# Probabilities times values in two float32r passes instead of float32 halves

## The chip, the cores and the metric

The kernel runs on one core of one Trainium2 chip. The metric is the device time of one execution in microseconds (us): lower is better. A run is repeated, and the median counts.

## The reference, cut to what matters

Two layers of a decoder trunk over 512 tokens of width 1024. In each layer four branches (a gated convolution, a sparse attention, a gated recurrence called HGRN2, and an attention to 256 memory tokens) start from one projection of the normalised input, are lifted to the full width, gated, summed and projected out; a feed-forward part follows. The change lies in the sparse attention. Each of its 8 heads has 64 dimensions, and all heads share one key and one value head:

```python
def one_block(args):                                # 128 queries
    qb, iqb, iwb, qpos = args
    ...
    _, sel = lax.top_k(score, topk)                 # 128 keys for each query
    ...
    logits = jnp.where(valid[:, :, None, :], logits, -jnp.inf)
    p = jax.nn.softmax(logits, axis=-1).astype(v.dtype)
    return jnp.einsum('bthk,btkd->bthd', p, v_sel)  # probabilities times values
```

Everything is float32, and the result has to be close to a float32 computation.

## The kernel before, in words

**Numbers in two parts.** Most matrix products take both operands apart into a high part, rounded to float32r, and a low part, what the rounding left. `mm3` (lines 267 to 272) adds three float32r products in PSUM: high by high, high by low, low by high. These are the lines L270 to L272 that fill the profile. Weights come in chunks of 1024 KB or 512 KB; for each half of a chunk ScalarE rounds the high part (`w_hi`) and VectorE subtracts (`w_lo`, line 225), at a high priority (`AHEAD`). All ScalarE activations go through the helper `A`, so they carry line 97 and are told apart by their tiles.

**The sparse attention.** `attend` (lines 688 to 721) makes eight steps in each layer: four blocks of 128 queries (t = 0 to 3), and two groups q of four heads for each. A step works on t+1 blocks of 128 keys, b = 0 to t, since later keys are masked. For each of its four heads it multiplies queries and keys (L685, L686, into a PSUM tile "at"), adds the bias that masks the keys not selected and takes the row's extreme value on VectorE (L698), takes the exponential and the sum on ScalarE, the reciprocal on VectorE (L701), and scales on ScalarE. Then, for each block of keys, four transposes on TensorE (L709) put the four heads' probabilities side by side in a PSUM tile "tr" of 512 columns, and ScalarE copies it to the SBUF tile `pt`. Last, the values: for each block and each half e of the four heads one float32 matmul of 256 columns (L715) with the values `vt` (128 keys by 64 dimensions) as weights; e = 0 writes partitions 0 to 63 of `pv`, e = 1 partitions 64 to 127, so that two heads lie above two others. In the profile each of these 80 matmuls is two instructions. ScalarE rounds `pv` to `y_hi`, VectorE subtracts to `y_lo` (line 720); the lift of branch B reads them. `vt` is written by ScalarE in `c_kv` (line 787), once for each block of tokens.

**What sets the order.** The kernel is written in generators: `weave` (line 851) runs one step of the lift of branch A or of the recurrence's values, then R2 = 3 attend steps, and so on. A scheduler in the tile framework then orders the instructions of each engine by its own model of time, with the waits put in as semaphores; from there each engine works through its own queue in order. Every PSUM or SBUF tile is one of a few buffers under a name, and a new tile waits until the one before it in the same buffer has been read: three "mm" tiles in PSUM for projections (MM_BUFS), three "tr", two "at". SBUF is reused as well: the pool of the recurrence (`hgrn`, line 853) lies where the attention's pools lay. The recurrence begins with `logits` (lines 873 to 881): six chunks of projections whose products with `r_b` on VectorE (L880) read an "mm" tile and write `zf`, `zq` and `zg`; the first `zf` tiles of each layer lie over the attention's `pt` buffers, in the kernel before as in the changed one.

Of the kernel before, what the change touches and what calls it, by code (L numbers as in the profile page):

```python
# [12 lines left out]
F32 = mybir.dt.float32  # L13
F32R = mybir.dt.float32r
I32 = mybir.dt.int32
U8 = mybir.dt.uint8
AF = mybir.ActivationFunctionType
OP = mybir.AluOpType
# [3 lines left out]
P = 128  # L22
S = 512
NT = S // P
# [4 lines left out]
HD = 64  # L29
# [20 lines left out]
HG = ["zzzHHlHlHzzzHHHHll", "zzzHHHHllzzzHHHllH"]  # L50
WARM = 14
LOOK = ["0000", "0010"]
W_BUFS, RAW_BUFS, G_BUFS, PT_BUFS, PR_BUFS = 3, 2, 4, 2, 5
MV_BUFS, MP_BUFS = 1, 3
R1, R2 = 6, 3

# [13 lines left out]
def hybrid_trunk(ctx: ExitStack, tc: tile.TileContext, x, mem, positions, norm_mix, w_in, conv_w,  # L70
# [3 lines left out]
    act, dve, pe, pool = nc.scalar, nc.vector, nc.tensor, nc.gpsimd  # L74

    consts = ctx.enter_context(tc.tile_pool(name="consts", bufs=1))
    start = ctx.enter_context(ExitStack())
# [12 lines left out]
    def A(dst, src, func, **kw):  # L90
        name = tables.get(func)
        if name is not None and name != table["set"]:
            load = act.preload_act_table_set(name)
            for u in table["users"]:
                tc.add_manual_dep(load.ins, u.name, order, reason="table set")
            table.update(set=name, load=load.ins, users=[])
        i = act.activation(dst, src, func, **kw)  # L97
        if name is not None:
            tc.add_manual_dep(i.ins, table["load"].name, order, reason="table set")
            table["users"].append(i.ins)  # L100
        return i
# [4 lines left out]
    def at_ps():  # L106
        return pat.tile([P, 512], F32, name="at", bufs=AT_BUFS)

    def tr_ps():
        return pat.tile([P, 512], F32, name="tr", bufs=TR_BUFS)  # L110

    def f(ap):
        return ap.bitcast(F32)
# [28 lines left out]
    ps = tr_ps()  # L142
# [16 lines left out]
    ps = tr_ps()  # L159
# [20 lines left out]
    for l in range(DEPTH):  # L180
        a = sp.tile([P, HD], F32, name=f"gq_raw{l}")
# [5 lines left out]
        b = consts.tile([P, HD], F32, name=f"gk{l}")  # L187
# [14 lines left out]
    def small(n, name="small", bufs=12):  # L202
        return consts.tile([P, 8], F32, name=name, bufs=bufs)[:, :n]
# [297 lines left out]
    def mixer(l, h, norms, cm, cf):  # L501
        mix = cm.enter_context(tc.tile_pool(name="mix", bufs=1, side="right"))
        r_t, r_b = norms()
# [172 lines left out]
        with pool_("dsa") as dp:  # L676
            qS = dp.tile([P, 8, S], F32R, name="qS")
            kS = (dp.tile([P, S], F32R, name="k_hi"), dp.tile([P, S], F32R, name="k_lo"))
            pool.memset(f(kS[1][HD:P, :]), 0.0)
            vt = dp.tile([P, NT, HD], F32, name="vt")  # L680
            biases = [causal_bias] + [dp.tile([P, (t + 1) * P], F32, name=f"bias{t}") for t in range(1, NT)]

            def dots(ps, q, k, hh, t, n):
                s = slice(t * P, (t + 1) * P)
                pe.matmul(ps, q[:, hh, s], k[0][:, :n], start=True, stop=False)  # L685
                pe.matmul(ps, q[:, hh, s], k[1][:, :n], start=False, stop=True)  # L686

            def attend(t, dp2, y_b):
                n = (t + 1) * P
                s = slice(t * P, (t + 1) * P)  # L690
                for q in range(2):
                    probs = []
                    for i in range(4):
                        ps = at_ps()[:, :n]
                        dots(ps, qS, kS, 4 * q + i, t, n)
                        p = dp2.tile([P, S], F32, name="prob", bufs=PR_BUFS)[:, :n]
                        mx, sm = small(1), small(1)
                        dve.tensor_tensor_reduce(out=p, in0=ps, in1=biases[t], scale=-1.0, scalar=-OFF * 4,  # L698
                                                 op0=OP.add, op1=OP.min, accum_out=mx)
                        A(p, p, AF.Exp, bias=mx, scale=-1.0, accum_out=sm)  # L700
                        dve.reciprocal(sm, sm)  # L701
                        A(p, p, AF.Copy, scale=sm)
                        probs.append(p)
                    pt = dp2.tile([P, NT, S], F32, name="pt", bufs=PT_BUFS)
                    for b in range(t + 1):
                        pp = tr_ps()
                        for e in range(2):
                            for i in range(2):
                                pe.transpose(pp[:, (2 * e + i) * P:(2 * e + i + 1) * P],  # L709
                                             probs[2 * i + e][:, b * P:(b + 1) * P], ident)  # L710
                        A(pt[:, b, :], pp, AF.Copy)
                    pv = tr_ps()[:, :2 * P]
                    for b in range(t + 1):
                        for e in range(2):
                            pe.matmul(pv[e * HD:(e + 1) * HD, :], vt[:, b, :], pt[:, b, e * 2 * P:(e + 1) * 2 * P],  # L715
                                      start=b == 0, stop=b == t)
                    pv = pv.rearrange("p (a b) -> p a b", b=P)
                    hi, lo = (y_b[x][:, 2 * q:2 * q + 2, s] for x in range(2))
                    A(hi, pv, AF.Copy)
                    dve.tensor_sub(lo, pv, f(hi))  # L720
                    yield

            with pool_("idx") as ip:
# [44 lines left out]
                def twin(ps, t, c0, norm, dst):  # L768
                    u = ip.tile([P, 2, HD], F32, name="twin", bufs=2)
                    A(u[:, 0, :], ps[:, c0:c0 + HD], AF.Copy, scale=r_t[:, t:t + 1])  # L770
                    if norm:
                        headnorm(u[:, 0:1], 1, gk_b[l])
                    rope(u[:, 0:1], 1, t)
                    dve.tensor_copy(u[:, 1, :], u[:, 0, :])
                    ps = tr_ps()[:, :P]
                    pe.transpose(ps, u.rearrange("p a b -> p (a b)"), ident)
                    s = slice(t * P, (t + 1) * P)
                    A(dst[0][:, s], ps, AF.Copy)
                    dve.tensor_sub(dst[1][0:HD, s], ps[0:HD], f(dst[0][0:HD, s]))

                def iq_part(ps, t, c0, heads, h0):
                    u = unit(ps, t, c0, heads)
                    rope(u, heads, t)
                    heads_T(iqS, h0, u.rearrange("p a b -> p (a b)"), heads, t)

                def c_kv(ps, t):
                    A(vt[:, t, :], ps[:, 64:128], AF.Copy, scale=r_t[:, t:t + 1])
                    twin(ps, t, 0, True, kS)
                    iq_part(ps, t, 128, 2, 0)

# [39 lines left out]
                def projections():  # L830
                    for c0, n, handle in ((C_DK, 256, c_kv), (C_DK + 256, 256, c_iq), (C_DK + 512, 200, c_last),
                                          (C_DQ, 256, c_q(0)), (C_DQ + 256, 256, c_q(1))):
                        w = wchunk(w_in[l][:, c0:c0 + n], KD, n)
                        for t in range(NT):
                            ps = mm_ps()[:, :n]
                            tokens(w, h, t, ps)
                            handle(ps, t)
                        yield
# [11 lines left out]
            with pool_("att", "left") as dp2:  # L850
                weave(chain(lift(0, y_a, merged), values(hv)), chain(*(attend(t, dp2, y_b) for t in range(NT))), R2)
# [229 lines left out]
    for l in range(DEPTH):  # L1081
        with ExitStack() as ctx_ffn:
            with ExitStack() as ctx_mix:
                h, ssq, xT = mixer(l, h, (lambda: (norm_token(ssq), norm_feature(ssq))) if l else (lambda: norms),
                                   ctx_mix, ctx_ffn)
            h, ssq = ffn(l, h, ssq, xT)
# [29 lines left out]
```

## Time and profile before

| | us |
|---|---|
| Median of three runs (2047.63 to 2047.9) | 2047.9 |
| The profiled execution | 2047.48 |
| Its span, first to last instruction | 2045.4 |
| TensorE busy | 2034.5 |
| VectorE busy | 1269.3 |
| ScalarE busy | 1017.5 |
| Sparse attention with what is woven into it, layer 0 | about 340 to 470 |
| The same, layer 1 | about 1300 to 1440 |

How to read the views: a row of the timeline gives the start in us from the beginning of the span, the duration, the engine, the line and the operation, the tiles (out<-in), the shapes, how many instructions it merges, and in brackets how long the engine had been idle and who ended that. A row of the groups gives line, engine, operation, tiles and shapes with the count, then busy us and the mean in ns, then the idle time just before, with its releasers. A row of the windows gives a stretch, its length, the busy time of each engine with its count (PE, PEld, DVE, ACT, POOL), the granted TensorE clock, the share of the DMA engines and GB/s. PE is TensorE, PEld its weight loads, DVE VectorE, ACT ScalarE, POOL GpSimd. Matmuls are pipelined and their ends are modelled: the distance of two starts says more than the printed duration.

### The profile page before, as it was taken

The page shows a single profiled execution, that of the slowest core. Times are in us where ns is not written, and L with a number is a line of the kernel's source. Part 1 is how long each engine was busy: PE and PEld are TensorE (multiplying, and loading weights), DVE is VectorE, ACT ScalarE, POOL GpSimd, SP SyncE. Part 2 cuts the span into 40 slices and gives each one's busy share as a digit, 9 for nine tenths or more (in the row PEclk, how much of TensorE's full clock was granted, in tenths as well). Part 3 has the DMA queues.
Part 4 walks back from the last instruction along what each step waited for, and adds up shares of the span by engine and source line. Part 5 has one row for each costly group of instructions (what it writes and reads, how often), then busy time and mean ns, then how long its engine had stood idle before and what let it go on. Part 6 is the DMA issues. An engine that isn't in the chain of part 4 may idle for free.

```text
span 2045.4 us, 26581 instructions
## 1 busy us (share of the span) xinstructions
PE 2034.5 (99%) x10348; PEld 1715.8 (84%) x10348; DVE 1269.3 (62%) x2507; ACT 1017.5 (50%) x1834; POOL 9.8 (0%) x33
## 2 busy tenths in 40 slices
PE   8999999999999999999999999999999999999999
PEld 8998988888888888888889898888888888888887
DVE  6779998547676544334457889963777754533442
ACT  7653655766665423223355456576767633322331
POOL 0000000000000000000000000000000000000000
PEclk9999999999999999999999999999999999999999
DMA  7632232223233232233243213322223322323322
GB/s 253 220 89 94 68 93 93 64 71 93 78 118 113 83 103 93 93 105 102 87 155 94 88 58 107 97 76 63 83 83 101 126 90 96 103 75 111 97 79 93
DMA packets 187709, 203.79 MB, mean 100 GB/s; under 512 B 4270, under 2 KB 176384, under 8 KB 187456
## 3 DMA queue, kind: packets, MB, share of 16 engines
q1 hardware_dynamic: 183872, 193.56, 29.8%
q10 hardware_dynamic: 3552, 8.41, 1.1%
q8 instruction: 81, 1.33, 0.3%
q14 instruction: 44, 0.36, 0.1%
q0 software_dynamic: 160, 0.13, 0.0%
HBM read 191.60 MB, written 10.49 MB: 99 GB/s over the span
## 4 chain that ended last, share of the span: by engine, by line
PE 99%; DMA 1%; DVE 0%; ACT 0%; SPq 0%; issue 0%; DVEq 0%
PE mm L270 30%; PE mm L272 30%; PE mm L271 30%; PE tr L715 1%; PE tr L709 1%; PE at L686 1%; PE at L685 1%; PE at L272 1%; PE at L270 1%; PE at L271 1%; DMA w_raw<-in_mem_w_kv_dram 1%; PE at L963 0%; PE at L937 0%; PE tr L653 0%; PE tr L754 0%; PE tr L972 0%
## 5 line engine op out<-in xcount | busy, mean ns | idle before, releaser
L270 PE MATMUL mm<-h_hi,w_hi 128*128 128x512 f32 x1664 | 653.0, 393 | 0.0
L271 PE MATMUL mm<-h_lo,w_hi 128*128 128x512 f32 x1664 | 652.1, 392 | 0.0
L272 PE MATMUL mm<-h_hi,w_lo 128*128 128x512 f32 x1664 | 650.1, 392 | 0.0
L225 DVE TENSOR_TENSOR w_lo<-w_raw,w_hi 128x1024 fp32r<-128x1024 f32 (+1 forms) x346 | 419.5, 1213 | 364.5 <-ACT w_hi L97 361.3
L97 ACT ACTIVATE w_hi<-w_raw 128x1024 fp32r<-128x1024 f32 (+1 forms) x346 | 363.4, 1051 | 460.8 <-PE mm L271 414.5
L272 PEld LDWEIGHTS mm<-h_hi,w_lo 128*128 128x128 f32 x1664 | 312.8, 188 | 64.8 <-issue 1.2
L270 PEld LDWEIGHTS mm<-h_hi,w_hi 128*128 128x128 f32 x1664 | 312.8, 188 | 64.5 <-issue 2.2
L271 PEld LDWEIGHTS mm<-h_lo,w_hi 128*128 128x128 f32 x1664 | 312.9, 188 | 63.8 <-issue 2.0
L272 PE MATMUL mm<-w_hi,h_lo 128*128 128x256 f32 (+1 forms) x448 | 128.2, 286 | 0.0
L271 PE MATMUL mm<-w_lo,h_hi 128*128 128x256 f32 (+1 forms) x448 | 127.0, 285 | 0.0
L270 PE MATMUL mm<-w_hi,h_hi 128*128 128x256 f32 (+1 forms) x448 | 127.0, 285 | 0.0
L271 PE MATMUL mm<-a_lo,w_hi 128*128 128x512 f32 x272 | 106.3, 391 | 0.0
L270 PE MATMUL mm<-a_hi,w_hi 128*128 128x512 f32 x272 | 106.0, 390 | 0.0
L272 PE MATMUL mm<-a_hi,w_lo 128*128 128x512 f32 x272 | 105.8, 391 | 0.0
L270 PE MATMUL mm<-y_hi,w_hi 128*128 128x512 f32 x256 | 101.4, 397 | 0.0
L272 PE MATMUL mm<-y_hi,w_lo 128*128 128x512 f32 x256 | 100.6, 393 | 0.0
L271 PE MATMUL mm<-y_lo,w_hi 128*128 128x512 f32 x256 | 100.3, 392 | 0.0
L272 PEld LDWEIGHTS mm<-w_hi,h_lo 128*128 128x128 f32 x448 | 85.8, 191 | 1.4 <-issue 0.8
L270 PEld LDWEIGHTS mm<-w_hi,h_hi 128*128 128x128 f32 x448 | 85.3, 191 | 1.2 <-issue 0.8
L271 PEld LDWEIGHTS mm<-w_lo,h_hi 128*128 128x128 f32 x448 | 85.6, 191 | 0.6
L97 ACT ACTIVATE a_hi<-fg 128x512 fp32r<-128x512 f32 x44 | 27.8, 633 | 109.4 <-DVE fg L1065 109.4
L97 ACT ACTIVATE prob<-prob,small 128x128 f32<-128x128 f32 (+3 forms) x128 | 69.2, 554 | 15.2 <-DVE small L698 14.6
(358 smaller groups left out, 2946.9 us busy)
## 6 DMA issues: line engine op xcount, KB each, us to landing
w_raw<-in_w_in_dram SPq DMA_DIRECT2D x72, 1024.0 KB, 5.3
w_raw<-in_ffn_w_up_dram SPq DMA_DIRECT2D x44, 1024.0 KB, 5.1
w_raw<-in_w_lift_dram SPq DMA_DIRECT2D x32, 512.0 KB, 3.5
w_raw<-in_ffn_w_down_dram SPq DMA_DIRECT2D x16, 1024.0 KB, 5.5
w_raw<-in_mem_w_kv_dram SPq DMA_DIRECT2D x8, 1024.0 KB, 5.4
w_raw<-in_w_out_dram SPq DMA_DIRECT2D x8, 1024.0 KB, 5.2
w_raw<-in_ffn_w_down_dram SPq DMA_DIRECT2D x10, 512.0 KB, 3.4
kv<-kv ACTq DMA_DIRECT2D x8, 512.0 KB, 3.2
```

The lines of the kernel that those rows point to most:

```text
L97: i = act.activation(dst, src, func, **kw)
L225: dve.tensor_sub(lo, raw[:, k:e], f(hi))
L270: pe.matmul(ps, ah, bh, start=first, stop=False)
L271: pe.matmul(ps, ah, bl, start=False, stop=False)
L272: pe.matmul(ps, al, bh, start=False, stop=last)
L685: pe.matmul(ps, q[:, hh, s], k[0][:, :n], start=True, stop=False)
L686: pe.matmul(ps, q[:, hh, s], k[1][:, :n], start=False, stop=True)
L709: pe.transpose(pp[:, (2 * e + i) * P:(2 * e + i + 1) * P], probs[2 * i + e][:, b * P:(b + 1) * P], ident)
L715: pe.matmul(pv[e * HD:(e + 1) * HD, :], vt[:, b, :], pt[:, b, e * 2 * P:(e + 1) * 2 * P], start=b == 0, stop=b == t)
```

## The change

The values are kept in two parts side by side, `vt[:, t, 0]` rounded to float32r and `vt[:, t, 1]` what the rounding left, together 128 columns of weights. Each block of transposed probabilities is taken apart as well, into `pt_hi` (ScalarE) and `pt_lo` (VectorE). Per block two float32r matmuls of 512 columns take the place of the float32 ones: all four heads at once, the first with `pt_hi`, the second with `pt_lo`. Partitions 0 to 63 of `pv` then hold the product with the values' high part and 64 to 127 that with the low part. ScalarE copies the lower half to SBUF (`pvl`), two VectorE additions add the halves and put two heads above the others again (`pva`), and `y_hi` and `y_lo` are made from `pva` in SBUF. The buffers of the transposed probabilities are now counted by block (four of each part) and no longer by step (two with room for four blocks).

```diff
-W_BUFS, RAW_BUFS, G_BUFS, PT_BUFS, PR_BUFS = 3, 2, 4, 2, 5
+W_BUFS, RAW_BUFS, G_BUFS, PT_BUFS, PR_BUFS = 3, 2, 4, 4, 5
...
-            vt = dp.tile([P, NT, HD], F32, name="vt")
+            vt = dp.tile([P, NT, 2, HD], F32R, name="vt")
...
-                    pt = dp2.tile([P, NT, S], F32, name="pt", bufs=PT_BUFS)
+                    pts = []
                     for b in range(t + 1):
                         pp = tr_ps()
                         for e in range(2):
                             for i in range(2):
                                 pe.transpose(pp[:, (2 * e + i) * P:(2 * e + i + 1) * P],
                                              probs[2 * i + e][:, b * P:(b + 1) * P], ident)
-                        A(pt[:, b, :], pp, AF.Copy)
-                    pv = tr_ps()[:, :2 * P]
-                    for b in range(t + 1):
-                        for e in range(2):
-                            pe.matmul(pv[e * HD:(e + 1) * HD, :], vt[:, b, :], pt[:, b, e * 2 * P:(e + 1) * 2 * P],
-                                      start=b == 0, stop=b == t)
-                    pv = pv.rearrange("p (a b) -> p a b", b=P)
+                        ph, pl = (dp2.tile([P, S], F32R, name=nm, bufs=PT_BUFS) for nm in ("pt_hi", "pt_lo"))
+                        A(ph, pp, AF.Copy)
+                        dve.tensor_sub(pl, pp, f(ph))
+                        pts.append((ph, pl))
+                    pv = tr_ps()
+                    for b, (ph, pl) in enumerate(pts):
+                        v = vt[:, b].rearrange("p a b -> p (a b)")
+                        pe.matmul(pv, v, ph, start=b == 0, stop=False)
+                        pe.matmul(pv, v, pl, start=False, stop=b == t)
+                    pv = pv.rearrange("p (e a b) -> p e a b", e=2, b=P)
+                    pvl = dp2.tile([HD, 2, 2, P], F32, name="pvl", bufs=1)
+                    A(pvl, pv[HD:P], AF.Copy)
+                    pva = dp2.tile([P, 2, P], F32, name="pva", bufs=1)
+                    for e in range(2):
+                        dve.tensor_add(pva[e * HD:(e + 1) * HD], pvl[:, e], pv[0:HD, e])
                     hi, lo = (y_b[x][:, 2 * q:2 * q + 2, s] for x in range(2))
-                    A(hi, pv, AF.Copy)
-                    dve.tensor_sub(lo, pv, f(hi))
+                    A(hi, pva, AF.Copy)
+                    dve.tensor_sub(lo, pva, f(hi))
                     yield
...
-                    A(vt[:, t, :], ps[:, 64:128], AF.Copy, scale=r_t[:, t:t + 1])
+                    A(vt[:, t, 0, :], ps[:, 64:128], AF.Copy, scale=r_t[:, t:t + 1])
+                    dve.scalar_tensor_tensor(vt[:, t, 1, :], ps[:, 64:128], r_t[:, t:t + 1], f(vt[:, t, 0, :]),
+                                             op0=OP.mult, op1=OP.subtract)
```

## The prediction

> **What bounds the kernel now.** I read the page first: span, engines, slices, then the chain that ended last.
>
> ```profile
> span 2045.4 us, 26581 instructions
> PE 2034.5 (99%) x10348; PEld 1715.8 (84%) x10348; DVE 1269.3 (62%) x2507; ACT 1017.5 (50%) x1834; POOL 9.8 (0%) x33
> ...
> PEclk9999999999999999999999999999999999999999
> ...
> PE 99%; DMA 1%; DVE 0%; ACT 0%; SPq 0%; issue 0%; DVEq 0%
> ```
>
> TensorE is busy throughout at full clock, and the chain is TensorE alone. A busy TensorE may still wait, since its ends are modelled, so I asked for the two stretches in which the sparse attention runs (columns: length, then busy time and count of PE, PEld, DVE, ACT, POOL).
>
> ```profile
> 340.00:470.00 130.00, 130.00 (x752) 106.09 (x751) 71.16 (x170) 91.33 (x193) 1.49 (x4) 1.00 0.25 78
> 1300.00:1440.00 140.00, 140.00 (x787) 114.30 (x787) 82.25 (x193) 94.54 (x194) 1.49 (x4) 1.00 0.23 71
> ```
>
> No idle TensorE in either, VectorE 55 to 59% busy, ScalarE 68 to 70%. So a microsecond of TensorE work removed here is a microsecond of the run, unless TensorE then waits for the slower engines. Third, the timeline, for what a matmul really occupies: the distance from one start to the next, not the printed duration.
>
> ```profile
> L715 PE MATMUL tr<-pt,vt x160: 378/380/432, 358.5 to 1430.5; 128*64 128x256 f32 x160
> ...
> 358.17 0.39 PE L271 MATMUL mm<-y_lo,w_hi 128*128 128x512 f32 x1
> 358.49 0.65 PE L715 MATMUL tr<-pt,vt 128*64 128x256 f32 x4
> 359.07 0.51 PE L272 MATMUL mm<-y_hi,w_lo 128*128 128x512 f32 x1
> 359.42 0.27 PE L709 MATMUL tr<-ident,prob 128*128 128x128 f32 x1
> ...
> 440.43 1.52 PE L715 MATMUL tr<-pt,vt 128*64 128x256 f32 x12
> 441.88 0.51 PE L270 MATMUL mm<-h_hi,w_hi 128*128 128x512 f32 x1
> ...
> 1430.27 0.65 PE L715 MATMUL tr<-pt,vt 128*64 128x256 f32 x4
> ...
> 1434.17 0.39 PE L270 MATMUL mm<-h_hi,w_hi 128*128 128x512 f32 x1
> 1441.88 0.39 PE L271 MATMUL mm<-h_lo,w_hi 128*128 128x512 f32 x1
> ```
>
> From 1434.17 to 1441.88 there are 34 starts of 512-column float32r matmuls: 0.227 us each, though each is printed with 0.39. L715 looks like 160 x 0.38 = 61 us, and is far less: a run of four (one block of 128 keys, both halves e) starts at 358.49 and the next matmul at 359.07, 0.58 us; a run of twelve takes 1.45. Each further block costs (1.45 - 0.58)/2 = 0.43.
>
> **The change, part by part.** *Removed from TensorE.* Around a run the neighbours are late as well: 358.17 to 358.49 is 0.32 instead of 0.227 and 359.07 to 359.42 is 0.35, so a run of one block costs 0.58 + 0.09 + 0.12 = 0.79. The 40 blocks stand in 30 runs (358.49 the first, 1430.27 the last): 24 of one block, 2 of two, 4 of three. With the neighbours 24 x 0.79 + 2 x 1.22 + 4 x 1.66 = 28.0 us; without them 24 x 0.58 + 2 x 1.02 + 4 x 1.45 = 21.8. Some runs stand two close together with transposes between and share the switch; I take **27**. *Added to TensorE:* two passes for each block, 80 of the form of L271, 80 x 0.227 = **18.2**. Net **-8.8**, bounds -3.6 and -9.8.
>
> *Added to ScalarE and VectorE.* The nearest rows:
>
> ```profile
> L657 DVE TENSOR_TENSOR mpt_lo<-tr,mpt_hi 128x512 fp32r<-128x512 f32 x16 | 11.0, 687 | 3.6 <-ACT mpt_hi L97 3.4
> L97 ACT ACTIVATE mpt_hi<-tr 128x512 fp32r<-128x512 f32 x16 | 9.5, 596 | 13.5 <-PE tr L653 13.1
> L97 ACT ACTIVATE pt<-tr 128x512 f32<-128x512 f32 x40 | 21.9, 592 | 4.7 <-PE tr L709 4.7
> L761 DVE TENSOR_TENSOR qS<-tr,qS 64x256 fp32r<-64x256 f32 x32 | 13.5, 423 | 1.0
> L97 ACT ACTIVATE y_hi<-tr 128x256 fp32r<-128x256 f32 x16 | 6.1, 379 | 16.0 <-PE tr L715 16.0
> L720 DVE TENSOR_TENSOR y_lo<-tr,y_hi 128x256 fp32r<-128x256 f32 x16 | 6.7, 421 | 8.7 <-ACT y_hi L97 8.5
> L880 DVE TENSOR_TENSOR zf<-mm,rstd 128x512 f32<-128x512 f32 x8 | 5.5, 689 | 9.2 <-PE tr L715 7.5 <-PE mm L272 1.5
> L519 DVE TENSOR_TENSOR gate<-mm,rstd 128x512 f32<-128x512 f32 x64 | 44.0, 687 | 28.8 <-PE mm L272 28.6
> ```
>
> Rounding pt to float32r costs what the copy cost (596 against 592 ns): nothing. In each layer VectorE gets 20 pt_lo of 0.69, 16 half adds of 0.42 and four small products for the values' low part (at most 0.42): 13.7 + 6.8 + 1.7 = 22 us, up to some 93 of 130. ScalarE gets 8 copies of pvl, 64x512, 0.60 by pt: 5 us, to 96 of 130. Both still fit; on the average they hide behind TensorE. The hiding has to hold for each wait, so I counted, in the built order of the changed kernel's instructions, the TensorE work (at its start distances) that stands between the last transpose of a block and the pass that needs it. It is 3.5 us or more for every block but those of the last attend step of each layer. Needed are 0.60 + 0.69 and the time in the two queues. Free, then, in 14 of 16 steps; cover gone, each late pt_lo costs up to its 0.69.
>
> Two pairs of projection matmuls now stand with 0.45 and 0.88 us of TensorE work between the end of one PSUM tile and its reuse, 1.36 being the least before; the product that frees it takes 0.69 after a matmul end of 0.39: **+0.7** together (0 to 1.5).
>
> *The end of the attention.* Here the change adds a wait. After the last pass ScalarE copies pvl, VectorE adds twice (pva), ScalarE rounds y_hi, VectorE subtracts y_lo; and in the changed order VectorE's next instruction behind y_lo is the first zf product of the HGRN stage. That product frees the PSUM tile for the matmul that stands right behind the last pass on TensorE; all three mm tiles are held until then. So this TensorE matmul, and all behind it, wait for the whole chain. Before, it was otherwise:
>
> ```profile
> 1426.61 0.68 DVE L880 TENSOR_TENSOR zf<-mm,rstd 128x512 f32<-128x512 f32 x1
> 1430.97 0.39 ACT L97 ACTIVATE y_hi<-tr 128x256 fp32r<-128x256 f32 x1 [5.05 <-PE tr L715]
> 1431.04 0.69 DVE L880 TENSOR_TENSOR zf<-mm,rstd 128x512 f32<-128x512 f32 x1 [3.75 <-PE tr L715]
> ```
>
> The first zf ran four microseconds ahead of the last L715, the second ahead of y_lo. Now, from the start of the last pass: matmul end and hand-over 0.44 (0.39, and 0.05 as from 1430.92 to 1430.97), pvl 0.60, two adds 0.42 + 0.34, y_hi 0.38, y_lo 0.34 until zf may start, zf 0.69, four hand-overs of 0.04 (1412.26 to 1412.30, below): 3.37. Unhindered the next matmul would start at 0.23. **3.1 us lost in each layer.** (The 0.34: a VectorE instruction that follows another starts some 0.08 before its end, 1412.18 against 1411.57 + 0.69.)
>
> In layer 1 the last step has no filler either: its sixteen transposes and eight passes stand nearly bare, behind the chain of the last head's probabilities.
>
> ```profile
> 1403.69 1.57 ACT L97 ACTIVATE pt<-tr 128x512 f32<-128x512 f32 x3 [0.59 <-PE tr L709]
> 1411.03 0.50 PE L686 MATMUL at<-k_lo,qS 128*128 128x512 f32 x1
> 1411.57 0.69 DVE L698 CUSTOM_DVE_ANT_0 prob<-at,bias 128x512 f32<-128x512 f32 x1 [2.19 <-PE at L686]
> 1412.18 0.08 DVE L698 DVE_READ_ACCUMULATOR2_ANT small<- 128x1 f32 x1
> 1412.30 0.72 ACT L97 ACTIVATE prob<-prob,small 128x512 f32<-128x512 f32 x1 [0.68 <-DVE small L698]
> 1412.93 0.19 ACT L97 ACTIVATION_READ_ACCUMULATOR prob<-prob,small 128x1 f32 x1
> 1413.65 0.15 DVE L701 RECIPROCAL small<-small 128x1 f32<-128x1 f32 x1
> ```
>
> From the start of that head's L686: minimum and exponential end at 2.0 (0.44 + 0.73 + 0.63 + 0.19), the scaled probabilities at 3.1 (a second pass of the same form, 0.72), since y_hi of the step before, 0.38, stands between; three pt_hi follow 0.49 apart, the first done at 4.1; pt_lo at 4.8, 5.4, 6.0; the fourth block's transposes wait for the first pt_lo to free a tr tile (4.9 to 5.3), its pt_hi is done at 6.1, its pt_lo at 6.8; last pass at 7.0. TensorE's own work in it is 0.23 + 0.46 + 15 x 0.11 + 7 x 0.227 = 3.9. Lost: **3.1** more. Layer 0 has thirteen matmuls as filler at this place; I put 0.3 there. The end of the attention thus costs 3.4 + 6.2 = **9.6** (bounds 0, if work turns up that the order hides, and 14).
>
> *The clock.* A TensorE that idles can lose its clock here:
>
> ```profile
> 8.00:12.00 4.00, 2.73 (x15) 1.49 (x15) 2.82 (x15) 2.93 (x13) 0.00 (x0) 1.00 1.04 370
> 12.00:16.00 4.00, 2.46 (x14) 2.26 (x15) 3.24 (x9) 3.97 (x8) 0.00 (x0) 0.86 1.02 406
> ...
> 14.51 0.28 PE L271 MATMUL mm<-w_lo,mt_hi 128*128 128x256 f32 x1
> 14.62 0.28 PE L272 MATMUL mm<-w_hi,mt_lo 128*128 128x256 f32 x1
> ...
> 17.84 0.41 PE L270 MATMUL mm<-w_hi,mt_hi 128*128 128x256 f32 x1
> 18.05 0.39 PE L271 MATMUL mm<-w_lo,mt_hi 128*128 128x256 f32 x1
> ```
>
> After some 2.8 us of idleness in eight (5.19 busy), starts go from 0.11 to 0.21 apart and back about 18.3, some 3.4 us at half clock: 1.7 us lost. Layer 1's end is about as idle as that (6.2 us in some eleven), layer 0's is shorter. I take **1.2**: one stretch, partly inside the wait (0 to 3.4).
> [...]
>
> **Sum.** -8.8 + 0.7 + 9.6 + 1.2 = +2.7 us on the profiled execution's 2047.48 (span 2045.4 and 2.1 around it; the median of the runs, 2047.9, is 0.4 above): **2050.2 us**. About 0.2% (4.1 us) is what a measurement of this kernel can tell from no change, so from 2043.8 to 2052.0 counts as the same.
>
> **Rivals.** (1) *TensorE's gain arrives nearly whole*: for it, no idle TensorE before and ample distance in 14 of 16 steps; against it, the order of zf. With ends at 0 to 4.5 us and a clock that holds: 2038.5 to 2043.8, say 2041.5. (2) *VectorE falls behind in the middle of the attention* (slower): its queue is in order, the weight casts and the gate products stand behind pt_lo, which stands behind ScalarE. Against it, 93 of 130 us; for it, runs of three pt_lo in a row. It decides once a queue is over 2.2 us late (3.5 less 1.3); with one pt_lo of 0.69 late in each of the 14 other steps, +9.7: 2060. (3) *The clock drops fully in both layers*, twice 1.7 instead of 1.2: 2052.4, just slower. (4) *The passes don't run at 0.227*, as float32r of this form: at twice that, +18: 2068. Against it, the 34 starts above.
>
> **How the numbers follow.** Forecast 0.46, its own range 2046 to 2052; rival 1 0.17; rival 2 0.18; rival 3 0.17; rival 4 0.02. Faster 0.17, same 0.46, slower 0.18 + 0.17 + 0.02 = 0.37. The range goes from 2042.5 (below it some 0.12 of rival 1) to 2057.0 (above it rival 4 and the full size of rival 2, about 0.06).
>
> **What would show it.** Passes 0.23 us apart; TensorE idle about 3 us twice in layer 1 and once in layer 0, ended by VectorE's zf; pt_lo near 0.69; TensorE without idle time in the other attend steps; a stretch below full clock behind layer 1's end. Wrong would be: zf ahead of pva or no idle time at the ends (rival 1), idle time in each step ended by pt_lo or by weight casts (rival 2).

## The result, and the profile after

The changed kernel takes **2054.5 us** (median of 7 runs, 2053.4 to 2055.0), the kernel before 2047.8 (7 runs, 2047.6 to 2048.0): ratio 1.0032, 95% interval 1.0022 to 1.0042. It is slower by 0.3%, 6.7 us. The profiled execution took 2054.43, 6.95 more than that of before. My forecast was 2050.2 with "no difference" as the likeliest case; 2054.5 lies inside the range and above the forecast's own (2046 to 2052).

The page of the changed kernel: span and engines, the chain that ended last, and the group of L270, whose last column is the idle time just before and who ended it.

```profile
span 2052.4 us, 26525 instructions
...
PE 2034.3 (99%) x10268; PEld 1725.5 (84%) x10268; DVE 1306.8 (64%) x2587; ACT 1027.5 (50%) x1850; POOL 10.0 (0%) x33
...
PE 98%; DMA 1%; DVE 0%; ACT 0%; issue 0%; SPq 0%; DVEq 0%; ACTq 0%
...
L270 PE MATMUL mm<-h_hi,w_hi 128*128 128x512 f32 x1664 | 653.4, 393 | 6.5 <-DVE zf L890 6.2
```

80 instructions fewer on TensorE, and yet the same busy time. Two things are new: 6.2 us in which TensorE waits for `zf`, and, in the windows of the same kernel (length, busy time and count of PE, PEld, DVE, ACT, POOL, then the granted clock), stretches at half clock. The short rows cut the two ends of the attention at the changes of the clock, which lie 3.41 us apart there (447.46 and 450.87, 1430.49 to 1440.73), and in steps of the same length beside them.

```profile
340.00:470.00 130.00, 126.88 (x709) 109.42 (x708) 89.21 (x206) 95.31 (x201) 1.56 (x4) 0.99 0.24 76
1300.00:1440.00 140.00, 134.42 (x726) 115.39 (x725) 99.92 (x233) 96.25 (x196) 1.61 (x4) 0.98 0.22 72
444.04:447.46 3.42, 0.30 (x2) 0.08 (x1) 1.98 (x5) 1.04 (x3) 0.57 (x3) 1.00 0.00 0
447.46:450.87 3.41, 3.41 (x8) 2.70 (x9) 2.02 (x4) 2.88 (x5) 0.00 (x0) 0.50 0.00 0
450.87:454.28 3.41, 3.41 (x16) 2.82 (x15) 2.96 (x4) 1.77 (x3) 0.00 (x0) 1.00 0.00 0
1427.08:1430.49 3.41, 1.22 (x7) 0.77 (x8) 1.89 (x5) 2.81 (x7) 0.00 (x0) 1.00 0.00 0
1430.49:1433.91 3.42, 3.42 (x11) 2.85 (x11) 1.68 (x3) 0.65 (x2) 0.89 (x2) 0.50 0.00 0
1433.91:1437.32 3.41, 0.51 (x3) 0.09 (x1) 1.74 (x4) 1.01 (x2) 0.73 (x3) 1.00 0.00 0
1437.32:1440.73 3.41, 3.24 (x8) 2.57 (x9) 1.96 (x4) 3.14 (x6) 0.00 (x0) 0.50 0.00 0
```

Three times a step in which TensorE hardly works (0.30, 1.22 and 0.51 us busy) is followed by one at a clock of 0.50. There TensorE is "busy" all the time and issues half as many matmuls: 8 in 447.46 to 450.87, 16 in the next. Each such stretch costs at most half of its 3.41 us, 1.7. The two long rows leave 3.12 and 5.58 us without TensorE work by the profile, and the waits in the next view (and layer 0's 3.12) are all of it. Who waits for whom at the end of layer 1 stands in the timeline of the same kernel:

```profile
1427.63 0.52 PE L709 MATMUL tr<-ident,prob 128*128 128x128 f32 x3 [0.87 <-DVE pva L725]
1428.60 0.55 PE L709 MATMUL tr<-ident,prob 128*128 128x128 f32 x3 [0.45 <-ACT prob L97]
1430.34 1.01 PE L709 MATMUL tr<-ident,prob 128*128 128x128 f32 x4 [1.19 <-DVE pt_lo L713]
...
1434.04 0.39 PE L719 MATMUL tr<-pt_lo,vt 128*128 128x512 f32 x1
1434.46 0.59 ACT L97 ACTIVATE pvl<-tr 64x512 f32<-64x512 f32 x1 [2.47 <-PE tr L719]
1435.09 0.84 DVE L725 TENSOR_TENSOR pva<-pvl,tr 64x256 f32<-64x256 f32 x2 [2.38 <-ACT pvl L97]
1435.96 0.42 ACT L97 ACTIVATE y_hi<-pva 128x256 fp32r<-128x256 f32 x1 [0.91 <-DVE pva L725]
1436.41 0.42 DVE L728 TENSOR_TENSOR y_lo<-pva,y_hi 128x256 fp32r<-128x256 f32 x1 [0.48 <-ACT y_hi L97]
1436.75 1.28 DVE L890 TENSOR_TENSOR zf<-mm,rstd 128x512 f32<-128x512 f32 x2
1437.49 0.79 PE L270 MATMUL mm<-h_hi,w_hi 128*128 128x512 f32 x1 [3.07 <-DVE zf L890]
```

The last pass starts at 1434.04, the next matmul at 1437.49: 3.45 us, where 0.23 is usual, so 3.2 lost. Layer 0 has the same picture (443.82 to 447.39, 3.3 lost). Layer 1 has three pieces more ahead of its passes, in the first three rows; by the distances of the starts they come to 1.03 + 0.61 + 1.36 = 3.0. (A matmul of 512 columns is drawn 0.39 us long where the next one starts 0.23 behind it, so the distances say somewhat more than the brackets.)

The sum for the profiled execution: waits 3.3 + 3.0 + 3.2 = 9.5; three stretches, at most 5.1; 0.5 at one reuse of a projection tile (1607.06 to 1607.77, 0.71 instead of 0.23); start-up 0.1. That is +15.2, and 6.95 came out, so the lighter product is worth at most 8.2 us of TensorE time. The stretch before layer 1's last pass cost less than 1.7: from the last four transposes to the last pass it took 3.70 us here and 2.32 in e1 below, where the clock was full, so 1.4; and the third began 0.17 us before its wait ended. With 4.7 for the three, the product is worth 7.8: **about 8 us**. It arrives, and more than all of it is given back at the two ends.

### The profile page after: what moved, and what is told of

Read it like the earlier page. It is cut to its first block, busy times and chain, and to the rows that moved or that the text cites. A ratio compares the mean times of both kernels' runs of the same rounds, so it can differ in the third digit from the quotient of the medians.

```text
span 2052.4 us, 26525 instructions
## 1 busy us (share of the span) xinstructions
PE 2034.3 (99%) x10268; PEld 1725.5 (84%) x10268; DVE 1306.8 (64%) x2587; ACT 1027.5 (50%) x1850; POOL 10.0 (0%) x33
## 4 chain that ended last, share of the span: by engine, by line
PE 98%; DMA 1%; DVE 0%; ACT 0%; issue 0%; SPq 0%; DVEq 0%; ACTq 0%
PE mm L270 30%; PE mm L271 30%; PE mm L272 30%; PE at L686 1%; PE at L685 1%; PE tr L709 1%; PE at L272 1%; PE at L270 1%; PE at L271 1%; DMA w_raw<-in_mem_w_kv_dram 1%; PE tr L719 0%; PE tr L718 0%; PE at L973 0%; PE at L947 0%; PE tr L653 0%; PE tr L762 0%
## 5 line engine op out<-in xcount | busy, mean ns | idle before, releaser
L270 PE MATMUL mm<-h_hi,w_hi 128*128 128x512 f32 x1664 | 653.4, 393 | 6.5 <-DVE zf L890 6.2
L270 PEld LDWEIGHTS mm<-h_hi,w_hi 128*128 128x128 f32 x1664 | 313.3, 188 | 72.5 <-DVE zf L890 6.9
L270 PE MATMUL mm<-w_hi,h_hi 128*128 128x256 f32 (+1 forms) x448 | 126.5, 284 | 0.0
L270 PE MATMUL mm<-a_hi,w_hi 128*128 128x512 f32 x272 | 105.9, 389 | 0.0
L270 PE MATMUL mm<-y_hi,w_hi 128*128 128x512 f32 x256 | 100.0, 392 | 0.0
L270 PEld LDWEIGHTS mm<-w_hi,h_hi 128*128 128x128 f32 x448 | 85.1, 191 | 1.0
```

The costliest lines, as they stand in the source:

```text
L270: pe.matmul(ps, ah, bh, start=first, stop=False)
```

## The experiments

The theory: the 8 us are real; they are given back (a) by the waits at the ends, because `zf` stands behind `pva` and `y_lo` on VectorE, and (b) by the stretches at half clock that follow. Rivals: the stretches come from something else (A); `pt_lo` on VectorE holds up the attention's steps in between (B). "As expected" and "a miss" are said of the time. "Before" in this section is the median beside each run, 2047.95 to 2048.08. The table gives four starts in the timelines; that of a layer's first output-projection matmul shows what was gained by then:

| us | before | changed | e1 | e2 | e4 | e6 |
|---|---|---|---|---|---|---|
| first matmul of layer 0's selection | 153.42 | 153.51 | 153.80 | 154.05 | 153.66 | 154.05 |
| first of layer 0's output projection | 648.81 | 649.68 | 645.76 | 645.57 | 644.75 | 649.48 |
| last product of layer 1's attention | 1430.55 | 1434.04 | 1428.78 | 1429.97 | 1435.39 | 1431.21 |
| first of layer 1's output projection | 1633.51 | 1640.54 | 1630.56 | 1631.13 | 1634.30 | 1638.42 |

**e1: the chain taken off the path.** The pool of the HGRN stage lies over the attention's, and in the built order `zf` came only behind the last VectorE instruction on a tile of that pool: with the change, `pva` and the `y_lo` that reads it. Here they lie elsewhere.

```diff
-                    pvl = dp2.tile([HD, 2, 2, P], F32, name="pvl", bufs=1)
+                    pvl = scratch512(S)[0:HD].rearrange("p (a b c) -> p a b c", a=2, b=2)
...
-                    pva = dp2.tile([P, 2, P], F32, name="pva", bufs=1)
+                    pva = scratch512(2 * P).rearrange("p (a b) -> p a b", a=2)
```

> The changed kernel with pvl and pva in the two scratch tiles (sq) of another pool instead of the attention's own pool, and nothing else. In the built order zf then stands ahead of the last pva and y_lo on VectorE and waits only for the last pass of the attention, whose pt tiles lie under it. Theory (the gain of the passes is real, and is given back at the two ends of the attention: TensorE waits for zf, and a half-clock stretch follows each of the two waits): the waits of 3.34 and 3.23 us shrink to about 1.0 each (zf itself, 0.64, and two hand-overs), 4.6 us less, and the two stretches behind them go, 1.7 each: about 2046.5 us. Rival A (the stretches come from something else): 2049.9. Rival B (the ends do not matter, pt_lo on VectorE holds up the steps in between): within 1 us of 2054.5.

Measured 2045.58 (11 runs; ratio to before 0.9988, interval 0.9979 to 0.9997): 8.9 less than the changed kernel, by two lines that change no arithmetic. The timeline has what is left of the waits for `zf`:

```profile
445.06 0.50 PE L270 MATMUL mm<-h_hi,w_hi 128*128 128x512 f32 x1 [0.50 <-DVE zf L890]
...
1429.73 0.50 PE L270 MATMUL mm<-h_hi,w_hi 128*128 128x512 f32 x1 [0.56 <-DVE zf L890]
```

0.72 us each by the starts, and in this execution no stretch at half clock after the start-up, not even behind the three pieces of layer 1 (granted clock 1.00 from 1300.00 to 1440.00). Rival B falls, A as well. This execution (2044.52) is one of three with a mean granted clock of 0.999; the other eight have 0.997 or 0.996 and take 2044.95 to 2046.84, so the median probably has a stretch in it.

**e2: `zf` free of the last passes too**: as e1, and eight spare tiles ahead of `logits`, which put `zf` over `qS`.

```diff
+            for nm in ("e", "ls", "cum", "cmr"):
+                for _ in range(HB):
+                    tmp(nm)
```

> As e1_scratch, and zf is also placed in memory over qS instead of over prob and pt, by eight spare tiles ahead of it, so that it need not wait for the last passes either. Theory: no wait for zf at either end, 6.6 us less than the changed kernel, and two stretches at half clock less, 3.4: about 2044.5 us. The waits of layer 1 ahead of its last passes (1.03, 0.61 and 1.36 us) and the stretch behind them stay. Rival A (stretches come from something else): 2047.9. Rival B (ends do not matter): within 1 us of 2054.5.

Measured 2044.56 (0.9982, 0.9973 to 0.9991), as expected. No wait for `zf` is left. The stretch behind layer 1's three pieces is there in this execution (windows of e2, and then the same place in e1):

```profile
1423.52:1426.94 3.42, 1.74 (x11) 1.12 (x11) 1.93 (x5) 2.52 (x5) 0.00 (x0) 1.00 0.00 0
1426.94:1430.35 3.41, 3.41 (x8) 2.68 (x9) 2.95 (x5) 0.60 (x1) 1.17 (x3) 0.50 0.00 0
```

```profile
1421.11:1424.53 3.42, 2.29 (x14) 1.57 (x12) 2.11 (x6) 2.21 (x5) 0.00 (x0) 1.00 0.00 0
1424.53:1427.94 3.41, 2.03 (x11) 1.48 (x12) 2.04 (x4) 2.31 (x5) 0.32 (x1) 1.00 0.00 0
1427.94:1431.35 3.41, 2.85 (x13) 2.03 (x12) 2.89 (x6) 2.11 (x4) 1.23 (x4) 1.00 0.00 0
```

The idle pieces are the same in both. In e2 two of them fall into one step of the clock (1.74 us busy), in e1 a border runs between them (2.29 and 2.03), and the clock stays at 1.00. (The borders of e1 are an estimate: they are counted on in steps of 3.41 us from its start-up, where its clock last changed. The estimate rests on the trace of the changed kernel, in which the changes of the clock lie whole numbers of such steps apart: at 3.413 us each the 430.08 us from 17.38 to 447.46 are 126 and the 979.62 from 450.87 to 1430.49 are 287.)

**e3: the waits kept, but not idle.** 14 repeats of the last pass, into a tile that nothing reads.

```diff
+                    if t == NT - 1 and q == 1:
+                        spare = tr_ps()
+                        for _ in range(FILL):
+                            pe.matmul(spare, v, pl, start=True, stop=True)
```

> The changed kernel with the last pass of each layer's attention repeated 14 times into a PSUM tile that nothing reads (14 x 0.23 = 3.2 us of TensorE work that the result does not need), standing in each wait for zf. The wait is the same for the kernel's own work, but TensorE is not idle in it. Theory: the time of the waits stays, the half-clock stretches behind them (447.5 in layer 0, 1437.3 in layer 1) go, 1.7 us each: about 2051.1 us. Rival A (the stretches do not come from the idle time): 2054.5 with the stretches where they were. If the repeats did not fit into the waits, up to 2061.

Measured 2051.10 (1.0016, 1.0007 to 1.0025), 3.4 less than the changed kernel, for 28 matmuls more. In its timeline the repeats fill the wait (and then the kernel's own work goes on at 0.23 to 0.24 us, full rate, in layer 1 from 1436.60 as well):

```profile
444.65 3.35 PE L724 MATMUL tr<-pt_lo,vt 128*128 128x512 f32 x14
447.95 0.50 PE L271 MATMUL mm<-h_hi,w_hi 128*128 128x512 f32 x1
448.29 0.40 PE L272 MATMUL mm<-h_lo,w_hi 128*128 128x512 f32 x1
448.53 0.40 PE L273 MATMUL mm<-h_hi,w_lo 128*128 128x512 f32 x1
```

Only the stretch behind layer 1's three pieces is left (1428.80 to 1432.21, granted clock 0.50; 1.00 in the next step and, in layer 0, from 442.60 to 449.42). This parts the two costs: waits about 6.5, their stretches 3.4.

**e4: more filler.** As e2, but `zf` lies in the pool of `hv`, in memory that the attention doesn't use, and `pt_lo` has three buffers to make the room. Projections of the next stage then run beside the last attention step.

```diff
-                            z = zs[nm, 2 * q + j] = tmp(nm, 2)
+                            z = zs[nm, 2 * q + j] = hvp.tile([P, S], F32, name=nm, bufs=2) if nm == "zf" else tmp(nm, 2)
```

> The changed kernel with pvl and pva in the scratch tiles, and zf in the pool of hv, in memory that the attention does not use (pt_lo with 3 buffers instead of 4 makes the room), zq, zg over qS. Two more projection tiles can then run while the last attention step's probabilities are made. Theory: no wait at either end and none ahead of the last passes of layer 1, so no half-clock stretch either; what is left is the TensorE saving of 8.6 less the 0.5 at the one reuse of a projection tile: 2039.5 to 2041 us. Rival B (pt_lo on VectorE holds up the steps in between): above 2046. If only the waits go and stretches stay: about 2045.

Measured 2049.02 (1.0006, 0.9997 to 1.0015): a miss, 8 us above the upper end of what was expected. The attention did as expected: no wait at either end, and layer 0 gained 4.3 us by its end (648.81 to 644.75, and 0.24 more that its start-up took longer). But the timeline of the next stage in layer 1 shows where it went:

```profile
1592.46 1.13 PE L986 MATMUL tr<-e,ones_h 128*128 128x512 f32 x2 [0.69 <-ACT e L97]
1598.62 1.22 PE L270 MATMUL mm<-y_hi,w_hi 128*128 128x512 f32 x2 [5.03 <-ACT y_hi L97]
```

The projections that were drawn forward had covered the last head of the recurrence. Without them TensorE stands for 0.85 and 5.40 us by the starts. Two steps at half clock come with it (0.50 from 1594.83 to 1601.65): the first lies inside the wait, the second has 3.03 us of work in it (a cost of at most 1.7). Together that is up to 8 us, about the size of the miss. Filler is a stock: what one wait takes, a later one lacks.

**e5: the heads of layer 1 in another order**, to bring filler behind the last head.

```diff
-HG = ["zzzHHlHlHzzzHHHHll", "zzzHHHHllzzzHHHllH"]
+HG = ["zzzHHlHlHzzzHHHHll", "zzzHHHHzzzHHHHllll"]
```

> As e4_filler, with the order of layer 1's next stage (the gated recurrence, its heads H and the lift units l) changed from zzzHHHHllzzzHHHllH to zzzHHHHzzzHHHHllll, so that the projections that now run early in the attention are made up for by lift work behind the last head. In e4_filler TensorE stood 0.85 and 5.40 us behind the last head (1591.5 and 1593.0 us), and a half-clock stretch of 6.83 us followed. Theory: those 6.2 us and the 3.4 that the stretch costs go, nothing else changes: 2049.0 - 9.6 = about 2039.4 us. Rival (the loss in e4_filler lies elsewhere, in the attention): 2049.

Measured 2051.73 (1.0020, 1.0011 to 1.0029): a miss again. The wait behind the last head is gone, and a longer one stands at the first heads, with two steps at half clock (0.50 from 1477.73 to 1484.56, the second with 2.92 us of work in it) and 1.64 more later:

```profile
1481.64 0.80 PE L270 MATMUL mm<-h_hi,w_hi 128*128 128x512 f32 x1 [7.47 <-DVE zg L894]
...
1512.57 0.50 PE L270 MATMUL mm<-h_hi,w_hi 128*128 128x512 f32 x1 [1.64 <-DVE gate L538]
```

**e6: the same moves on the kernel before**, which has no `pvl` and `pva`: `zf` in the pool of `hv`, the spare tiles, and

```diff
-HG = ["zzzHHlHlHzzzHHHHll", "zzzHHHHllzzzHHHllH"]
+HG = ["zzzHHlHlHzzzHHHHll", "zzzHHHHzzzHHHHllll"]
```

> The kernel before the change with the same moves as e5_filler_late: zf in the pool of hv, zq and zg over qS, the new order of layer 1's stage. Theory: the kernel before has no wait at the ends of the attention and no half-clock stretch behind them, so the moves give nothing: 2047 to 2049 us, and e5_filler_late against this one is what the change itself is worth, 8 to 9 us. Rival (the moves are themselves a gain, whatever is done to probabilities times values): near 2040.

Measured 2052.57 (1.0025, 1.0015 to 1.0035): slower than expected, by the new order of the heads, which costs this kernel two waits as well:

```profile
1483.60 0.50 PE L270 MATMUL mm<-h_hi,w_hi 128*128 128x512 f32 x1 [1.13 <-DVE zg L884]
...
1518.94 0.50 PE L270 MATMUL mm<-h_hi,w_hi 128*128 128x512 f32 x1 [1.99 <-DVE zg L884]
```

As a control it serves as far as the heads of layer 1: from the selection of layer 0 to the last product of layer 1's attention it runs like before (0.63 later at the first, 0.66 at the last), so up to there the moves of memory are worth nothing without the change. The other aim, to read the worth of the change from e5 against e6, failed: 0.8 instead of 8 to 9, since the new order costs e5 more than e6 (by the starts 7.83 + 1.79 and up to 1.7 at half clock, against 1.29 + 2.14). With these taken out of the 0.8, some 8.6 are left, an estimate.

**e7: no low part of the probabilities** (their low part is left out of the product).

```diff
-                        dve.tensor_sub(pl, pp, f(ph))
...
-                        pe.matmul(pv, v, pl, start=False, stop=b == t)
```

> The changed kernel without the passes over the low part of the probabilities: pt_lo isn't made and L719 isn't issued, so the low part is left out of the product. Everything else is as changed (split values, halves added through pvl and pva). Theory: 40 passes at 0.227 are 9.1 us of TensorE; the waits for zf at the ends stay (their chain doesn't hold pt_lo), with the stretches behind them: 2054.5 - 9.1 = about 2045.4 us. A rival by which pt_lo on VectorE also holds up the steps in between: 40 x 0.69 = 27.6 us of VectorE less, and 5 to 10 us more than 9.1 gained, below 2040.

Measured 2043.71 (0.9981, 0.9972 to 0.9990), its profiled execution 2045.05: 10.8 and 9.4 less than the changed kernel for 40 passes, 9.1 by the count (why the medians differ by 1.7 more than the count is not shown). Rival B's 2040 and less is not reached. The waits at the ends are unchanged (3.34 by the starts in both layers).

**e8: `pt_lo` on the kernel before.**

```diff
+                        pl = dp2.tile([P, S], F32R, name="pt_lo", bufs=2)
+                        dve.tensor_sub(pl, pp, pt[:, b, :])
```

> The kernel before the change with one subtraction of 128x512 on VectorE added for each block of the attention, as the change adds it (40 in all, 0.69 us each), into a tile that nothing reads. Theory: VectorE has room for it in the attention, and the order at the ends keeps zf ahead of the last y_lo: 2047.5 to 2049 us. Rival B (pt_lo on VectorE holds up the attention's steps): the 14 steps that my prediction's rival counted at 0.69 each, about 2057.

Measured 2048.26 against 2047.95 (1.0002, 0.9993 to 1.0010): 27 us of VectorE work cost 0.3, and 2.0 at the interval's end, where rival B asked for 9. Nothing waits for what it writes, so the run tests VectorE's load alone; that no pass waits for `pt_lo` in the other steps is shown by the changed kernel, which has no idle TensorE there. With both, rival B is out.

**e9: the parts that worked.** Layer 0 as e4, layer 1 as e2, heads in the old order (the edit is shown against e4).

```diff
-                            z = zs[nm, 2 * q + j] = hvp.tile([P, S], F32, name=nm, bufs=2) if nm == "zf" else tmp(nm, 2)
+                            z = zs[nm, 2 * q + j] = hvp.tile([P, S], F32, name=nm, bufs=2) if nm == "zf" and l == 0 else tmp(nm, 2)
```

> The changed kernel with pvl and pva in the scratch tiles and pt_lo with 3 buffers; in layer 0 zf lies in the pool of hv as in e4_filler, in layer 1 over qS as in e2_scratch_clear, and the order of the heads is as before. Theory: layer 0 as in e4_filler (4.3 us gained by its end), layer 1 as in e2_scratch_clear (its waits of 3.0 us in the last attention step and the stretch behind them stay): 0.4 below e2_scratch_clear, 2044.1 us. Rival (the loss of e4_filler comes with zf in the pool of hv or the third buffer of pt_lo, not with layer 1's missing filler): 2046 or more.

Measured 2043.98 (0.9978, 0.9969 to 0.9987), as expected: the fastest version that computes only what is needed, 4.1 below the kernel before and 10.5 below the changed one. Its runs fall in two groups, 2042.7 to 2043.2 (four, mean granted clock 0.998) and 2043.9 to 2044.5 (seven, 0.997).

**e10: layer 1's three pieces kept busy**: e9 with 11 repeats of an earlier pass in the last step.

```diff
+                    if l and t == NT - 1 and q == 1:
+                        spare = tr_ps()
+                        for _ in range(FILL):
+                            pe.matmul(spare, v, pl, start=True, stop=True)
```

> As e9_mixed, with 11 repeats of an earlier pass (11 x 0.23 = 2.5 us that the result does not need) in layer 1's last attention step, where TensorE stands for 3.0 us in three pieces. Theory: the three pieces end when the probabilities come, so the repeats cost at most 0.5, and without the idle time no half-clock stretch follows: between 2042.4 and 2043. Rival (that stretch isn't from these waits): 2044.1 to 2044.6.

Measured 2043.66 (0.9979, 0.9970 to 0.9988), 0.7 above the expectation's upper end: the stretch is gone in the profiled execution, but the repeats cost more than the 0.5 allowed. From the last head's start (line 686 in e1, 687 here) to the last pass this step takes 8.17 us (1420.71 to 1428.88) and 7.30 in e1 (1421.48 to 1428.78), both at a granted clock of 1.00: 0.87 for the repeats, whose 2.5 us stand where only 1.03 + 0.61 were idle. The windows of the step:

```profile
1422.17:1425.59 3.42, 3.19 (x21) 2.59 (x19) 1.41 (x4) 2.17 (x6) 0.00 (x0) 1.00 0.00 0
1425.59:1429.00 3.41, 2.44 (x12) 1.84 (x12) 2.90 (x5) 1.77 (x4) 0.88 (x2) 1.00 0.00 0
1429.00:1432.41 3.41, 3.36 (x16) 2.56 (x15) 2.25 (x6) 3.06 (x6) 0.68 (x3) 1.00 0.00 0
```

The eleven runs lie within 0.55 us, those of e9 within 1.8. This fits a stretch that comes and goes in e9, as do the clocks of its two groups; but the start-up's own half-clock time is in these means, so it is a sign and not shown.

**e11: 8 repeats instead of 14** in e3.

```diff
-FILL = 14
+FILL = 8
```

> As e3_fill with 8 repeats instead of 14: the waits for zf keep 1.5 and 1.4 us of idle time. In the traces so far a half-clock stretch began at the end of a span of 3.41 us in which TensorE stood 2.0 us or more, and none after spans with 1.4 or less. Theory: no stretch behind either wait, as in e3_fill, about 2051.1 us. Rival (any wait of over 1 us brings a stretch): 2054.5.

Measured 2050.76 (1.0012, 1.0003 to 1.0021), as expected and like e3. Layer 0 stood for 1.47 us and kept its clock (1.00), which speaks against the rival; in layer 1 the stretch behind the three pieces took two steps, the repeats ran in part at half clock, and only 0.69 of the wait was left idle, so layer 1 tests nothing here:

```profile
445.23:448.65 3.42, 2.12 (x10) 1.43 (x9) 2.81 (x6) 1.33 (x4) 0.00 (x0) 1.00 0.00 0
448.65:452.06 3.41, 3.41 (x17) 2.79 (x16) 2.01 (x4) 3.41 (x6) 0.00 (x0) 1.00 0.00 0
1424.86:1428.27 3.41, 1.79 (x12) 1.04 (x10) 1.87 (x6) 2.81 (x6) 0.00 (x0) 1.00 0.00 0
1428.27:1431.68 3.41, 2.50 (x8) 2.22 (x9) 2.58 (x4) 1.71 (x4) 0.53 (x1) 0.50 0.00 0
1431.68:1435.10 3.42, 3.42 (x9) 2.65 (x9) 0.72 (x2) 0.59 (x1) 1.09 (x3) 0.50 0.00 0
```

**e12: the longer end alone, on the kernel before.**

```diff
+                    pvl = dp2.tile([P, 2 * P], F32, name="pvl", bufs=1)
+                    A(pvl, pv, AF.Copy)
+                    pva = dp2.tile([P, 2 * P], F32, name="pva", bufs=1)
+                    for e in range(2):
+                        o = slice(e * HD, (e + 1) * HD)
+                        dve.tensor_copy(pva[o], pvl[o])
+                    pv = pva.rearrange("p (a b) -> p a b", b=P)
```

> The kernel before the change with the change's longer end alone: the product goes by ScalarE into pvl, by two VectorE copies of 64x256 into pva, both in the attention's pool, and y_hi and y_lo are made from pva. TensorE's work is as before. In the built order zf then stands behind the last y_lo, as in the changed kernel; 8 matmuls of 0.227 are left behind the last product. Theory: the chain from the last product to zf is about 2.9 us (3.45 in the changed kernel, less 0.17 and 0.34 for the smaller copies), 1.8 of it covered: a wait of about 1 us in each layer, too short for a half-clock stretch: 2049.5 to 2050.5. Rival (the longer end is hidden): 2047.5 to 2048.3.

Measured 2050.32 (1.0012, 1.0003 to 1.0021), as expected; its timeline shows the waits, which came with no stretch behind them:

```profile
449.59 0.50 PE L270 MATMUL mm<-h_hi,w_hi 128*128 128x512 f32 x1 [0.58 <-DVE zf L886]
...
1435.42 0.50 PE L270 MATMUL mm<-h_hi,w_hi 128*128 128x512 f32 x1 [0.58 <-DVE zf L886]
```

0.74 each by the starts. The other 0.8 of the 2.2 us isn't in one place, and I didn't follow it up.

## Why the prediction was four microseconds short

- **TensorE's saving, -8.8: right, somewhat large.** The sum above leaves 7.8 to 8.2; e4's layer 0, with no wait in it, gained 4.3. A full-rate pass comes 0.23 us after the other (rival 4 out).
- **The work on VectorE and ScalarE at nothing: right.** e8 prices `pt_lo` at 0.3 (2.0 at the interval's end), and no idle TensorE shows in the other 14 steps (rival 2 out).
- **Two reuses of a projection tile, +0.7: right** (0.5, at one of the two).
- **The ends of the attention, +9.6: right, and for the reason given.** 3.3, 3.0 and 3.2 against 3.4 (with the 0.3 of layer 0), 3.1 and 3.1; the releasers are the ones named, and e1 and e2 give the time back when `zf` is let past. One of the three pieces is released by `pva` of the step before, which I had not counted there; the whole chain of the last head holds all the same, 7.3 from its start to the last pass in e1 against 7.0. In layer 0 it is in part luck: the 0.3 for the last step did not come, and the wait for `zf` was 0.2 longer than 3.1.
- **The clock, +1.2: this step failed.** I took one stretch, partly inside a wait and in layer 1 alone, bounds 0 to 3.4. There are three, 4.7 to 5.1 us in all, above the upper bound. e3 shows that idle time brings these: with TensorE busy in the same waits, the two behind the ends are gone (starts 0.23 to 0.24 us apart there, 0.43 in the changed kernel's stretch from 1437.32). With 4.7 to 5.1 in place of 1.2 my sum gives 2053.7 to 2054.1 for an execution measured at 2054.4. Rival 3 had the mechanism, with two stretches.
- Why I undersized it: I compared the waits with the start-up by shares over 8 us ("layer 0's is shorter"), not by steps of 3.41 us. Layer 0's one wait of 3.3 fills such a step almost alone (0.30 us busy). Nor is 6.2 us in eleven "about as idle" as 2.8 in eight: it is 56% against 35%.

How long such a loss lasts, as measured: behind the waits the clock stood at 0.50 for 3.41 us in the changed kernel, e2 and e3, and for two times that in e4, e5, e7 (layer 0, 442.78 to 449.60) and e11. The same idle pieces brought it in e2 and not in e1.

What stays open: the kernel before has an order in layer 1's last stage that just covers its heads. Neither e4 nor e5 found one that also lends filler to the attention, so layer 1's 3.0 us of waits remain in e2 and e9.

## What to carry to other kernels

When a change shortens the bound engine's work, look at where the stage ends: the step that no longer has filler, and the first instruction of the next stage that stands behind a longer chain on another engine's queue. A scratch tile's pool can decide that order: two lines here were worth 8.9 us. Price an idle spell of the bound engine twice, as time and as clock, and count the clock in its own steps (3.41 us in these traces).

## What the runs showed of the hardware

- **A step need not be idle throughout.** Behind the waits inside the kernels, full-clock steps of 3.41 us with 0.30, 0.51 and 1.22 (changed kernel), 1.74 (e2) and 1.79 us (e11) of busy TensorE were followed by half clock (0.50); those with 2.03 and 2.29 (e1, whose borders are an estimate) and 2.12 (e11) were not (1.00). The idle time need not be in one piece: in e2's step the two pieces are 0.45 and 1.20 us by the profile.
- **The printed busy time is no threshold.** In the start-up of the kernel before, the step from 4.63 with 1.54 us busy kept the clock (1.00), and the one from 11.46 with 1.63 was followed by half clock (0.50); in that of the changed kernel the one from 7.14 was, with 1.99. What e11's expectation reads from the traces therefore holds for the waits inside the kernels alone. The ends behind this busy time are modelled; what the clock goes by stays open.
- **The way back.** At half clock, steps with 2.26 us busy (changed kernel, start-up, from 10.55), 2.50 (e11) and 2.58 (e7, layer 0, from 442.78) were followed by another step at half; those with 2.83 (e3), 3.20 (changed kernel, start-up, from 13.97) and 3.41 (changed kernel, from 447.46) by full clock, and so was the one with 3.24 in its layer 1.
- **Scatter.** The sets of runs of the kernel before, e8, e10 and e12 each lie within 0.3 to 1.4 us; those of the changed kernel and of the other experiments, which have longer waits, spread over 1.7 to 2.9 us, as much as one stretch or more. That the clock makes all of this is not shown.
